# Delta rule in blocks of 64 columns on alternating halves of TensorE, with TensorE in program order

## The chip, the cores and the metric

One core of one Trainium2 chip runs the whole program. The metric is the device time of one execution in microseconds (us), lower is better.

## The reference

Batch 1, 512 tokens, width 1024, float32. A first block of two layers (MLA attention and gated linear attention) is followed by a second block of two layers; the change lies only in the mixer of the second block. Cut to what it computes there:

```python
proj = h @ w_in                                  # h = rms_norm(x)
# dilated attention over 8 heads of 64: three patterns, merged by softmax of their log sums
# delta rule: 4 heads, dk = dv = 128, chunks C = 64, N = 8 chunks
qkv = silu(causal_dwconv(dn_qkv, dn_conv_w))     # q, k, v of the delta rule
beta = sigmoid(dn_b); g = -exp(a_log) * softplus(dn_a + dt_bias)
q = q * rsqrt(sum(q*q) + EPS) * K**-0.5;  k = k * rsqrt(sum(k*k) + EPS)
g = cumsum(g, -1)                                # within each chunk of 64
decay = exp(where(tril, g_i - g_j, -inf))
A = where(strict, (beta k) k^T * decay, 0);  T = (I + A)^-1
u = T @ (v * beta);  w = T @ (beta * k * exp(g));  qk = (q k^T) * decay
for each chunk:                                  # state is 128 x 128 a head
    v_new = u_i - w_i @ state
    o = (q_i * exp(g)) @ state + qk_i @ v_new
    state = state * exp(g_last) + (k_i * exp(g_last - g))^T @ v_new
mix = concat([attn, rms_norm(o) * silu(z)]) @ w_out
```

## The kernel before

**Dense work.** Each large product is done as three fp32r matmuls per 128x128x512 block (`mm3`, L178 to L181: high times high, low times high, high times low), eight blocks deep. The weights come over SP's DMA queue (`wr<-in_w`, L140), are rounded by ACT (L143) and their rest taken by DVE (L144). `t_out` gives a 128-column slice with the channels on the partitions, `n_out` a 128-token slice with the tokens there.

**The mixer `mix2`**, once per layer: z projections (`ev`), the log decays (L948, L949 and what leads to them), then the **main stage**: k, q and v of the four heads with `t_out` (`dn`), their convolution and silu (`conv_silu_`, ACT and DVE), the attention's q and k with `n_out` and rope, and its v (`v_rows`). Between these dense matmuls lie the small f32 groups of the delta rule. TensorE takes an f32 matmul as two passes, and the trace counts passes. The groups, for each head four 128x128 tiles (a tile holds two chunks on its diagonal, the rest is masked away):

- `gB` (L1011), running decays; `G` (L1020), k times k; A goes to HBM (`dA`, L1025).
- 16x16 diagonal blocks of all heads come back in one layout (L1037), DVE inverts them in 30 steps (L1043, L1045), they go to `dT` (L1047). These DMAs are ACT's.
- `q_rows`: ACT squares all of q (L1053), TensorE sums over the partitions against a column of ones (L1056), then q times k (L1060). Both groups write bank 3 ("tr").
- `merges`: T is loaded (L1109) and flipped (L1114), then two rounds of X = A'T (L1120) and T -= T X (L1125); u (L1129) and w (L1137).
- the scan over 8 chunks: `pv` (L1151), `qv` (L1154), `dS` (L1160), one half of a tile's 128 rows or columns at a time, all four heads on the same half; `po` (L1167) once in two chunks.

**The attention stage** follows: `scores` (L1220, L1221), softmax on DVE and ACT, `weigh` (flip of the weights), `values` (L1243, two heads in turn on the two column halves), `finish`, `project`. The products of two of the four `v_rows` are issued here ("ps_mo").

**What sets the order.** The Tile scheduler orders each engine's instructions by the priorities that the program gives: `flush` runs postponed small work (`late`) at the priority of that place, the whole of `merges` stands 600 steps ahead, `scores` at its own place. So single dense matmuls stand between, and inside, the small groups.

Of the kernel before, what the change touches and what calls it, by code (L numbers as in the profile page):

```python
# [37 lines left out]
def shape_consts():  # L38
# [5 lines left out]
    for d in (3, 2, 1, 0):  # L44
# [10 lines left out]
    m16 = (i // 32 == j // 32) & (i % 32 >= 16) & (j % 32 < 16)  # L55
    m32 = same & (i % 64 >= 32) & (j % 64 < 32)
# [3 lines left out]
        "mask_ls": np.where(same & (i > j), 0.0, NEG),  # L60
        "mask_u": np.where(same & (i <= j), 0.0, NEG),
# [29 lines left out]
def body(ctx, tc, a, out, plan, n1=LAYERS, n2=LAYERS, dbg=None):  # L91
# [115 lines left out]

    def n_out(w, xk, c, evac, k_outer=False, then={}):
        nk = len(w)
        if k_outer:  # L210
            pss = [bank("mm") for _ in range(NT)]
            for k in range(nk):
                for t in range(NT):
                    mm3(pss[t][:, :c], cut(xk[k], tsl(t)), w[k], k == 0, k == nk - 1)
            for t in range(NT):
                evac(t, pss[t])
            return
        for t in range(NT):
            ps = bank("mm")
            for k in range(nk):  # L220
                mm3(ps[:, :c], cut(xk[k], tsl(t)), w[k], k == 0, k == nk - 1)
            if late:
                late.pop(0)()
            evac(t, ps)
            if t in then:
                then[t]()

    def t_out(w, xk, evac):
        nk = len(w)
        ps = bank("mm")  # L230
        for k in range(nk):
            mm3(ps, w[k], xk[k], k == 0, k == nk - 1)
        flush()
# [620 lines left out]
    def z_w(l, j):  # L854
        return take_n("w_in_2", l, np.concatenate([rng2(6)[j * 256:j * 256 + 256], rng2(7 + j)]), range(KT))

    def block2(xt, xd, pss):
        with ExitStack() as c2:
# [15 lines left out]
            dA = [dr.tile([P, 4, SEQ], F32, name=f"dA{l}", bufs=1) for l in range(LAYERS)]  # L874
            dT = [dr.tile([P, 4, SEQ], F32, name=f"dT{l}", bufs=1) for l in range(LAYERS)]
            zt = tmp()
            nc.gpsimd.memset(zt, 0.0)
            for l in range(n2):
                for h in range(4):
                    nc.sync.dma_start(dT[l][:, h], zt)  # L880
# [5 lines left out]
    def mix2(l, rt, xt, par, row, dA, dT, pss):  # L886
# [3 lines left out]
        with ExitStack() as cm:  # L890
            pm = pool(f"pm{l}", cm)
            deal(mm=(0, 1, 2), tr=(3,), d=(4, 5, 6, 7), pv=(4,), qv=(5,), dS=(6,), po=(7,),
# [10 lines left out]
            def dt():  # L903
                return gt("dt", 6)
# [4 lines left out]
            def f16(ap):  # L909
                return ap.rearrange("p h t -> p (h t)")  # L910

# [8 lines left out]
            for j in range(2):  # L920
                def ev(t, ps, j=j):
                    zs = z[t][:, tsl(j, 256)]
                    silu2(ps[:, :256], zs, 256)
                    nc.vector.scalar_tensor_tensor(heads(zs, 2), heads(zs, 2), 0.5, mid(d_gain, 2), ALU.mult, ALU.mult)
                    nc.vector.tensor_copy((bb, aa)[j][:, :, t], ps[:, 256:260])
# [21 lines left out]
            ps = bank("d")  # L947
            nc.tensor.matmul(ps[:, 0:16], cc("tri"), f16(graw), start=True, stop=True)  # L948
            nc.tensor.matmul(ps[:, 16:32], cc("same"), f16(graw), start=True, stop=True)  # L949
            gc, ngc, kd, eg = s16("gc"), s16("ngc"), s16("kd"), s16("eg")  # L950
            nc.vector.tensor_copy(f16(gc), ps[:, 0:16])
            nc.vector.tensor_scalar(f16(ngc), ps[:, 0:16], -1.0, None, ALU.mult)
            nc.vector.tensor_tensor(f16(kd), ps[:, 16:32], f16(gc), ALU.subtract)
            nc.scalar.activation(kd, kd, AF.Exp)
            nc.scalar.activation(eg, gc, AF.Exp)


            def conv_silu(m, ps, dst):
                with tc.high_priority(offset=0):
                    conv_silu_(m, ps, dst)  # L960

            def conv_silu_(m, ps, dst):
# [7 lines left out]
                nc.vector.scalar_tensor_tensor(dst, th, 1.0, acc, ALU.add, ALU.mult)  # L970
# [15 lines left out]
            A, ET, kN, qT = rows(set4("A")), rows(set4("ET")), rows(set4("kN")), rows(set4("qT"))  # L986
            kT = [gt("kT", 4) for _ in range(4)]
# [14 lines left out]
            for h in range(4):  # L1002
                dn(4 + h, kT[h])
                late.append(lambda h=h: k_rows(h))


            decl = pm.tile([P, 4, 8], F32, name="decl")
            for h in range(4):
                gB = bank("d")
                for t in range(NT):  # L1010
                    nc.tensor.matmul(gB[:, tsl(t)], graw[:, h, t:t + 1].to_broadcast([P, P]), cc("tri"),  # L1011
                                     start=True, stop=True)
                nc.scalar.activation(decl[:, h], gB.rearrange("p (n c) -> p n c", c=64)[:, :, 63], AF.Exp)
                d = dt()
                nc.vector.scalar_tensor_tensor(v4(d), v4(gB), -1.0, mid(cc("mask_ls"), NT), ALU.mult, ALU.add)
                nc.vector.tensor_tensor(v4(ET[h]), v4(gB), mid(cc("mask_u"), NT), ALU.add)
                flush()
                G = bank("d")
                for t in range(NT):
                    nc.tensor.matmul(G[:, tsl(t)], kT[h][:, tsl(t)], kT[h][:, tsl(t)], start=True, stop=True)  # L1020
                for t in range(NT):
                    nc.scalar.activation(d[:, tsl(t)], d[:, tsl(t)], AF.Exp, bias=gc[:, h, t:t + 1])
                    nc.vector.scalar_tensor_tensor(A[h][:, tsl(t)], G[:, tsl(t)], sa[:, h, t:t + 1], d[:, tsl(t)],
                                                   ALU.mult, ALU.mult)
                nc.scalar.dma_start(dA[:, h], A[h])  # L1025
                for t in range(NT):
                    nc.scalar.activation(ET[h][:, tsl(t)], ET[h][:, tsl(t)], AF.Exp, bias=ngc[:, h, t:t + 1])


            def diag(d, u):  # L1030
                row_ = 4 * SEQ
                return bass.AP(d.tensor, d.offset + u * (16 * row_ + 16), [[P, 16], [row_, 16], [1, 16]])

            LR = dt().rearrange("p (b r c) -> p b r c", b=2, r=16)
            Lb, Rb = LR[:, 0], LR[:, 1]
            for u in range(8):
                nc.scalar.dma_start(Lb[16 * u:16 * u + 16], diag(dA, u))  # L1037
            nc.sync.dma_start(Rb, a["eye16"])
            tmpb = tmp(256).rearrange("p (r c) -> p r c", r=16)
            for j in range(15):  # L1040
                n = 15 - j
                tv = tmpb[:, :n, :j + 1]
                nc.vector.tensor_tensor(tv, Lb[:, j + 1:, j:j + 1].to_broadcast([P, n, j + 1]),  # L1043
                                        Rb[:, j:j + 1, :j + 1].to_broadcast([P, n, j + 1]), ALU.mult)
                nc.vector.tensor_tensor(Rb[:, j + 1:, :j + 1], Rb[:, j + 1:, :j + 1], tv, ALU.subtract)  # L1045
            for u in range(8):
                nc.scalar.dma_start(diag(dT, u), Rb[16 * u:16 * u + 16])  # L1047
# [3 lines left out]
            def q_rows(h):  # L1051
# [3 lines left out]
                for t in range(NT):  # L1055
# [396 lines left out]
```

## Time and profile before

| | |
|---|---|
| median of 3 runs | 2131.49 us (2128.54 to 2132.91) |
| the profiled execution | 2130.51 us, of which the span of the trace 2128.4 us |
| PE busy | 2037.4 us (96%) |
| PE weight loads | 1685.4 us (79%) |
| DVE, ACT, POOL busy | 1279.2 (60%), 959.2 (45%), 194.9 us (9%) |
| mean DMA rate | 98 GB/s |
| granted TensorE clock, mean | 0.996 |

TensorE is busy in nearly all of the span, the other engines in about half. The records of single matmuls overlap, so this document takes the time of a group of matmuls from its first start to the start of what follows it.

### The profile page before, as it was taken

How to read it: one execution, taken by the hardware profiler on the slowest of the kernel's cores; microseconds unless marked ns; L12 is line 12 of the kernel's file. 1: busy time of each engine (PE TensorE's matmuls, PEld its weight loads, DVE VectorE, ACT ScalarE, POOL GpSimd, SP SyncE). 2: the span in 40 equal slices, each digit the busy share in tenths (PEclk: the TensorE clock that was granted, in tenths of full speed). 3: DMA queues.
4: the chain of work that ended last, by engine and by line, in shares of the span. 5: the costliest groups of instructions: out<-in, count | busy, mean ns of one | idle time of the engine just before them, and what ended most of it. 6: DMA issues, size and time to landing. Idle time of an engine off the chain costs nothing.

```text
span 2128.4 us, 28253 instructions
## 1 busy us (share of the span) xinstructions
PE 2037.4 (96%) x10792; PEld 1685.4 (79%) x10792; DVE 1279.2 (60%) x2218; ACT 959.2 (45%) x1805; POOL 194.9 (9%) x337
## 2 busy tenths in 40 slices
PE   7899999999999899999999999999999999999998
PEld 6687878778877888777788888878887678888886
DVE  6667655667844676575666425567757646662364
ACT  4745444635634553255544324346333654442342
POOL 1110001111000111200200000021112020000001
PEclk9999999999999999999999999999999999999999
DMA  5232233322133531141633333243211244332332
GB/s 170 85 92 70 70 109 118 104 80 87 44 127 103 173 95 58 45 114 51 188 109 99 92 96 99 70 152 113 79 55 50 75 146 142 99 97 92 99 99 89
DMA packets 74038, 209.41 MB, mean 98 GB/s; under 512 B 16624, under 2 KB 17648, under 8 KB 73392
## 3 DMA queue, kind: packets, MB, share of 16 engines
q1 hardware_dynamic: 62896, 202.89, 31.1%
q10 hardware_dynamic: 11008, 4.72, 0.9%
q8 instruction: 85, 1.39, 0.3%
q14 instruction: 49, 0.40, 0.1%
HBM read 182.16 MB, written 17.04 MB: 94 GB/s over the span
## 4 chain that ended last, share of the span: by engine, by line
PE 75%; DVE 7%; ACT 6%; DMA 5%; issue 3%; POOL 3%; POOLq 0%; SPq 0%; ACTq 0%; DVEq 0%
PE ps_mm L180 19%; PE ps_mm L181 18%; PE ps_mm L179 18%; DMA wr<-in_w 4%; DVE wl L144 2%; PE ps_tr L274 2%; ACT wh L143 2%; PE ps_o L1243 1%; ACT xn L296 1%; PE ps_mo L179 1%; PE ps_mo L180 1%; PE ps_pt L274 1%; PE ps_mo L181 1%; POOL r2h L297 1%; PE ps_pv L1151 1%
## 5 line engine op out<-in xcount | busy, mean ns | idle before, releaser
L144 DVE TENSOR_TENSOR wl<-wr,wh 128x1024 fp32r<-128x1024 f32 (+4 forms) x304 | 360.7, 1189 | 395.4 <-ACT wh L143 389.7
L143 ACT CAST wh<-wr 128x1024 fp32r<-128x1024 f32 (+4 forms) x304 | 309.3, 1019 | 357.1 <-PE ps_mm L181 151.3
L180 PE MATMUL ps_mm<-wl,xh 128*128 128x512 f32 (+2 forms) x736 | 282.6, 385 | 9.3 <-DVE wl L144 9.2
L181 PE MATMUL ps_mm<-x2h,wl 128*128 128x512 f32 (+1 forms) x768 | 285.5, 372 | 0.0
L180 PE MATMUL ps_mm<-x2l,wh 128*128 128x512 f32 (+1 forms) x768 | 285.4, 372 | 0.0
L179 PE MATMUL ps_mm<-x2h,wh 128*128 128x512 f32 (+1 forms) x768 | 285.4, 372 | 0.0
L179 PE MATMUL ps_mm<-wh,xh 128*128 128x512 f32 (+2 forms) x736 | 282.7, 386 | 2.1 <-ACT wh L143 1.7
L181 PE MATMUL ps_mm<-wh,xl 128*128 128x512 f32 (+2 forms) x736 | 280.9, 382 | 0.0
L180 PEld LDWEIGHTS ps_mm<-wl,xh 128*128 128x128 f32 x736 | 139.9, 190 | 37.5 <-DVE wl L144 15.0
L181 PEld LDWEIGHTS ps_mm<-x2h,wl 128*128 128x128 f32 x768 | 144.7, 188 | 25.1
L180 PEld LDWEIGHTS ps_mm<-x2l,wh 128*128 128x128 f32 x768 | 144.7, 188 | 25.0
L179 PEld LDWEIGHTS ps_mm<-x2h,wh 128*128 128x128 f32 x768 | 144.7, 188 | 24.9
L179 PEld LDWEIGHTS ps_mm<-wh,xh 128*128 128x128 f32 x736 | 139.5, 190 | 28.8 <-ACT wh L143 4.8
L181 PEld LDWEIGHTS ps_mm<-wh,xl 128*128 128x128 f32 x736 | 139.7, 190 | 23.3 <-issue 0.7
L1336 DVE SCALAR_TENSOR_TENSOR rt<-ps_mm,par,rt 128x511 f32<-128x511 f32 (+1 forms) x176 | 131.3, 746 | 3.0
L179 PE MATMUL ps_mm<-xh,wh 128*128 128x512 f32 x320 | 127.0, 397 | 0.9 <-DVE rp L358 0.9
L180 PE MATMUL ps_mm<-xl,wh 128*128 128x512 f32 x320 | 126.4, 395 | 0.0
L181 PE MATMUL ps_mm<-xh,wl 128*128 128x512 f32 x320 | 126.4, 395 | 0.0
L297 POOL TENSOR_SCALAR r2h<-ss 128x1 f32<-128x1 f32 x48 | 18.9, 393 | 995.0 <-ACT th L296 759.6
L180 PE MATMUL ps_mm<-wl,hh 128*128 128x512 f32 x224 | 89.1, 399 | 0.6 <-DVE wl L144 0.5
L179 PE MATMUL ps_mm<-wh,hh 128*128 128x512 f32 x224 | 88.2, 395 | 0.3 <-ACT wh L143 0.3
L181 PE MATMUL ps_mm<-wh,hl 128*128 128x512 f32 x224 | 88.0, 394 | 0.0
(401 smaller groups left out, 3798.3 us busy)
## 6 DMA issues: line engine op xcount, KB each, us to landing
wr<-in_w SPq DMA_DIRECT2D x270, 512.0 KB, 3.6
gain<-in_gain SPq DMA_DIRECT2D x13, 512.0 KB, 6.3
wr<-in_w SPq DMA_DIRECT2D x14, 384.0 KB, 3.1
x<-in_x SPq DMA_DIRECT2D x8, 512.0 KB, 5.9
wm<-gqk SPq DMA_DIRECT2D x32, 128.0 KB, 2.3
xd<-x SPq DMA_DIRECT2D x8, 512.0 KB, 2.6
xs<-xd SPq DMA_DIRECT2D x8, 512.0 KB, 3.9
xs<-xm SPq DMA_DIRECT2D x8, 512.0 KB, 4.6
```

The lines of the kernel that those rows point to most:

```text
L143: nc.scalar.copy(hi[:, :n], raw[:, :n])
L144: nc.vector.tensor_tensor(lo[:, :n], raw[:, :n], hi[:, :n].bitcast(F32), ALU.subtract)
L179: nc.tensor.matmul(ps, l[0], r[0], start=start, stop=False)
L180: nc.tensor.matmul(ps, l[0], r[1], start=False, stop=False)
L181: nc.tensor.matmul(ps, l[1], r[0], start=False, stop=stop)
L274: nc.tensor.transpose(ps[:w, tsl(j)], src[:, tsl(j, w)], ident)
L296: nc.scalar.activation(junk[i], halves[i], AF.Square, accum_out=ss[:, i:i + 1])
L297: nc.gpsimd.tensor_scalar(r[:, i:i + 1], ss[:, i:i + 1], 1.0 / D, r[:, 0:1] if i else EPS, ALU.mult, ALU.add)
L1151: nc.tensor.matmul(pv[rs, tsl(h)], wT[h][:, cs], S[:, h], start=True, stop=True)
L1243: nc.tensor.matmul(o[tsl(h % 2, 64), tsl(h // 2)], av[:, j, tsl(h, 64)], p_[:, tsl(i * c + j)], start=j == 0, stop=j == qt)
L1336: nc.vector.scalar_tensor_tensor(acc[:, j:], ps[:, :SEQ - j], par[:, w0 + 3 * m + 2 - j:w0 + 3 * m + 3 - j], acc[:, j:], ALU.mult, ALU.add)
```

## The change

All of it lies in `mix2`, in both layers. PE's order is the program's own there (`manual_schedule`): `later(n, fn)` postpones a small group until n more blocks of three dense matmuls have been issued, `tick` counts them, `settle` drains the list. The delta rule uses 64x64 blocks: heads 0 and 1 keep their time halves, heads 2 and 3 have the two halves of each tile swapped, so that two heads' blocks can lie on different halves of the array. Consecutive matmuls of a group take turns between the half F (partitions 0 to 63) and B (64 to 127), most with a PSUM bank for each half. The log decays become two accumulating 64-column matmuls per block; T is written and loaded in both orientations (16 DMAs in place of 8, on SP's queue, as all of the inversion's), so it is no longer flipped after loading; the sum of q's squares is taken by flipping q and four accumulating Squares of ACT; all four `v_rows` lie in the main stage; the attention's units start their second step one unit later, and take `w_out` and the flips of the delta rule's output earlier.

```diff
+    def later(n, fn):
+        steps.append([n, fn])
+    def tick():
+        for s in steps:
+            s[0] -= 1
...
             for k in range(nk):
                 mm3(ps[:, :c], cut(xk[k], tsl(t)), w[k], k == 0, k == nk - 1)
+                tick()
...
+            cm.enter_context(tc.manual_schedule(engines={mybir.EngineType.PE}))
-            deal(mm=(0, 1, 2), tr=(3,), d=(4, 5, 6, 7), pv=(4,), qv=(5,), dS=(6,), po=(7,),
+            deal(mm=(0, 1, 2), tr=(3,), d=(4, 5, 6, 7), pv=(4,), qv=(5,), dS=(6, 7), po=(3,),
...
+            later(6, decays)
...
+            def log_decays(g):
+                M = bank("d")
+                for i in range(8):
+                    h, t, o = 2 * g + i // NT, i % NT, M[:, tsl(i, 64)]
+                    for p in HF:
+                        nc.tensor.matmul(o[p], ngraw[:, h, t:t + 1].to_broadcast([P, 64]), tri[:, p], start=True, stop=False)
+                    for p in HF:
+                        nc.tensor.matmul(o[p], tri[:, p], graw[:, h, t:t + 1].to_broadcast([P, 64]), start=False, stop=True)
...
+            def k_scores(g):
...
+                        nc.tensor.matmul(G[p, tsl(i, 64)], kc, kc, start=True, stop=True)
...
+                for d, b in zip(dT, (Rb, Lb)):
+                    for u in range(8):
+                        nc.sync.dma_start(diag(d, u), b[16 * u:16 * u + 16])
+                merge_start()
...
             def q_rows(h):
-                sq = tmp()
-                nc.scalar.activation(sq, qT[h], AF.Square)
-                ps = bank("tr")
+                sq, ps = tmp(), flip(qT[h])
                 for t in range(NT):
-                    nc.tensor.matmul(ps[:, t:t + 1], sq[:, tsl(t)], ones[:, 0:1], start=True, stop=True)
-                nc.vector.tensor_copy(ssq[:, h], ps[:, 0:NT])
-                ps = bank("tr")
+                    nc.scalar.activation(sq[:, tsl(t)], ps[:, tsl(t)], AF.Square, accum_out=ssq[:, h, t:t + 1])
+                ps = bank("tr")[:, :256]
                 for t in range(NT):
-                    nc.tensor.matmul(ps[:, tsl(t)], kT[h][:, tsl(t)], qT[h][:, tsl(t)], start=True, stop=True)
+                    for u, p in enumerate(HF):
+                        nc.tensor.matmul(ps[p, tsl(t, 64)], chunks(kT[h])[:, t, u], chunks(qT[h])[:, t, u],
+                                         start=True, stop=True)
...
+            def halves(f):
+                ps = bank("d"), bank("d")
+                for i in range(8):
+                    for p, b in zip(HF, ps):
+                        f(i, p, b)
+                return tuple(zip(HF, ps))
...
+                def left(A_):
+                    for p, ps in halves(lambda i, p, b: nc.tensor.matmul(
+                            b[p, tsl(i, 64)], A_[p, tsl(i, 64)], TT[p, tsl(i, 64)], start=True, stop=True)):
+                        nc.scalar.copy(X[p], ps[p])
...
+                for i, fn in enumerate((lambda: left(As[0]), right, turn, lambda: left(As[1]), last, values_, keys)):
+                    later(wait + 4 * i, fn)
...
+            order = [(g, 2 * g + j) for j in range(2) for g in range(2)]
...
+                for g, h in order:
+                    nc.tensor.matmul(pv[HF[u ^ g], tsl(h)], chunks(wT_[:, h])[:, t, u ^ g], S[:, h], start=True, stop=True)
...
+                    later(2, lambda: update(n))
...
+                later(3, lambda: chunk(n + 1))
...
+            k_heads()
+            for h in range(4):
+                dn(h, qT[h])
+                later(10, lambda h=h: q_rows(h))
...
-            D1, D2, IW = 2, 5, 9
-            IV = [2 + 2 * i for i in range(NT - 2)]
-            IO = range(6, 6 + 4)
+            D1, D2, IW = 3, 5, 0
+            IO = range(2, 2 + NT)
```

In the changed code the three dense lines are L181 to L183, and flips are L298. The order of PE's instructions in three places (one row is one kind of matmul; an f32 one counts once here, and as two passes in the trace):

The rows of q for one head in the main stage, before (`ps_tr` is bank 3, `th` the squares):

```order
L1056 MATMUL ps_tr<-ones,th 128x1 x4
L180 MATMUL ps_mm<-xl,wh 128x512
L181 MATMUL ps_mm<-xh,wl 128x512
L179 MATMUL ps_mm<-xh,wh 128x512
L180 MATMUL ps_mm<-xl,wh 128x512
L181 MATMUL ps_mm<-xh,wl 128x512
L1060 MATMUL ps_tr<-qT,kT 128x128 x4
```

and now:

```order
L182 MATMUL ps_mm<-xl,wh 128x512
L183 MATMUL ps_mm<-xh,wl 128x512
L298 MATMUL ps_tr<-ident,qT 128x128 x4
L1145 MATMUL ps_tr<-qT,kT 64x64 x8
L181 MATMUL ps_mm<-xh,wh 128x512
```

The two groups on bank 3 were five dense matmuls apart, and now follow each other.

One step of the scan, before (`ps_dS` is the state's update, `ps_pv` and `ps_qv` the products with the state; dense ones stand between):

```order
L1160 MATMUL ps_dS<-vn,kN 128x128 x4
L181 MATMUL ps_mm<-wh,xl 128x512
L179 MATMUL ps_mm<-wh,xh 128x512
L180 MATMUL ps_mm<-wl,xh 128x512
L181 MATMUL ps_mm<-wh,xl 128x512
L1151 MATMUL ps_pv<-S,A 64x128 x4
L1154 MATMUL ps_qv<-S,qT 64x128 x4
```

and now:

```order
L1278 MATMUL ps_pv<-S,A 64x128 x4
L1283 MATMUL ps_qv<-S,qT 64x128 x4
L181 MATMUL ps_mm<-wh,xh 128x512
L182 MATMUL ps_mm<-wl,xh 128x512
L183 MATMUL ps_mm<-wh,xl 128x512
L298 MATMUL ps_tr<-ident,cv 128x128 x4
L181 MATMUL ps_mm<-wh,xh 128x512
L182 MATMUL ps_mm<-wl,xh 128x512
L183 MATMUL ps_mm<-wh,xl 128x512
L1298 MATMUL ps_dS<-vn,kN 128x128 x4
```

The groups keep their size; whole blocks of three dense matmuls stand between them.

The first units of the attention, before (`ps_s` are scores, `ps_pt` flipped weights, `ps_mo` the attention's v of tokens 256 to 511):

```order
L181 MATMUL ps_mo<-wh,xl 128x512
L179 MATMUL ps_mo<-wh,xh 128x512
L180 MATMUL ps_mo<-wl,xh 128x512
L274 MATMUL ps_pt<-ident,dt 128x128
L181 MATMUL ps_mo<-wh,xl 128x512
L179 MATMUL ps_mo<-wh,xh 128x512
L180 MATMUL ps_mo<-wl,xh 128x512
L1220 MATMUL ps_s<-ET,qT 128x256
L181 MATMUL ps_mo<-wh,xl 128x512
```

and now:

```order
L1389 MATMUL ps_s<-kN,A 128x256
L1390 MATMUL ps_s<-vs,A 128x256
L1389 MATMUL ps_s<-ET,qT 128x256
L1390 MATMUL ps_s<-lo,qT 128x256
L298 MATMUL ps_po<-ident,uN 128x128 x4
L1389 MATMUL ps_s<-kN,A 128x256
L1390 MATMUL ps_s<-vs,A 128x256
L1389 MATMUL ps_s<-ET,qT 128x256
L1390 MATMUL ps_s<-lo,qT 128x256
L298 MATMUL ps_pt<-ident,dt 128x128 x2
```

No dense matmul is left between the first scores.

## Rows read from the trace of the kernel before

**Rows 1.** The page: busy time and share of the span of each engine.

```profile
PE 2037.4 (96%) x10792; PEld 1685.4 (79%) x10792; DVE 1279.2 (60%) x2218; ACT 959.2 (45%) x1805; POOL 194.9 (9%) x337
```

**Rows 2.** Stretches: main and attention stage of layer 0, main of 1, the attention's start.

```profile
core 0: us, PE busy (x) PEld busy (x) DVE busy (x) ACT busy (x) POOL busy (x), PEclk, DMA share, GB/s
733.00:935.00 202.00, 195.28 (x1144) 163.19 (x1145) 137.80 (x254) 84.20 (x176) 33.53 (x39) 1.00 0.24 72
935.00:1012.00 77.00, 74.07 (x467) 56.47 (x466) 44.98 (x145) 45.41 (x112) 0.19 (x1) 1.00 0.31 84
1446.70:1642.00 195.30, 190.02 (x1115) 158.24 (x1116) 136.33 (x250) 80.59 (x173) 34.83 (x39) 1.00 0.22 66
...
940.00:960.00 20.00, 17.17 (x99) 12.72 (x97) 12.87 (x57) 13.85 (x40) 0.00 (x0) 1.00 0.52 138
```

**Rows 3.** Timeline of PE, full-width groups: start, us, line, tiles, passes.

```profile
826.27 1.13 PE L1120 MATMUL ps_d<-dt 128*128 128x128 f32 x8
827.15 0.47 PE L180 MATMUL ps_mm<-wl,xh 128*128 128x512 f32 x1
...
830.45 0.60 PE L274 MATMUL ps_d<-ident,dt 128*128 128x128 f32 x4
830.88 1.06 PE L1120 MATMUL ps_d<-dt 128*128 128x128 f32 x8
```

**Rows 4.** Timeline of PE: sums of q's squares against ones, and dense matmuls behind.

```profile
789.03 0.95 PE L1056 MATMUL ps_tr<-ones,th 128*128 128x1 f32 x8
789.84 0.48 PE L180 MATMUL ps_mm<-xl,wh 128*128 128x512 f32 x1
790.15 0.39 PE L181 MATMUL ps_mm<-xh,wl 128*128 128x512 f32 x1
790.38 0.40 PE L179 MATMUL ps_mm<-xh,wh 128*128 128x512 f32 x1
```

**Rows 5.** Timeline of PE: the scan, all heads on one half.

```profile
876.82 1.16 PE L1160 MATMUL ps_dS<-vn,kN 64*128 64x128 f32 x8
877.90 0.50 PE L181 MATMUL ps_mm<-wh,xl 128*128 128x512 f32 x1
878.24 0.40 PE L179 MATMUL ps_mm<-wh,xh 128*128 128x512 f32 x1
...
879.03 1.09 PE L1151 MATMUL ps_pv<-S,A 128*64 128x128 f32 x8
879.96 1.04 PE L1154 MATMUL ps_qv<-S,qT 128*64 128x128 f32 x8
880.92 0.50 PE L179 MATMUL ps_mm<-wh,xh 128*128 128x512 f32 x1
```

**Rows 6.** Timeline of PE, first block: matmuls that take turns between row halves.

```profile
80.66 0.27 PE L547 MATMUL ps_sf<-wm 64*128 64x128 f32 x1
80.67 0.27 PE L547 MATMUL ps_sb<-wm 64*128 64x128 f32 x1
80.77 0.27 PE L547 MATMUL ps_sf<-wm 64*128 64x128 f32 x1
```

**Rows 7.** Timeline of PE, attention: turns between column halves.

```profile
993.85 1.09 PE L1243 MATMUL ps_o<-cv,av 128*64 128x128 f32 x16
994.88 0.50 PE L1220 MATMUL ps_s<-ET,qT 128*128 128x512 f32 x1
```

**Rows 8.** Timeline of ACT: a weight cast, and the first Squares of k's rows.

```profile
746.12 1.05 ACT L143 CAST wh<-wr 128x1024 fp32r<-128x1024 f32 x1 [0.63 <-PE ps_mm L180]
...
748.74 0.31 ACT L996 ACTIVATE th<-kN 128x128 f32<-128x128 f32 x1
...
749.05 0.29 ACT L996 ACTIVATE th<-kN 128x128 f32<-128x128 f32 x1
```

**Rows 9.** Timeline: PE at the decays; DVE at the inversion's first step.

```profile
733.31 0.37 PE L948 MATMUL ps_d<-graw,cst 128*128 128x16 f32 x2 [1.20 <-issue]
...
782.17 0.19 DVE L1043 TENSOR_TENSOR th<-dt 128x15 f32<-128x15 f32 x1 [0.72 <-DMA dt<-dA]
```

More of the change, by code (lines that the diff above doesn't have):

```diff
@@ L984, in rows @@
                 return [ap[:, i] for i in range(4)]
[L986 to L987 removed]
+            wT_, ET_, kN, qT = set4("A"), set4("ET"), rows(set4("kN")), rows(set4("qT"))
+            nc.gpsimd.memset(ET_, 0.0)
+            kT = rows(set4("kT"))
+            EA = set4("lo")
+            E, A = EA[:, 0:2], EA[:, 2:4]
             ssk, ssq = s16("ssk"), s16("ssq")
@@ new lines, in values_ @@
+                def values_():
+                    for j in range(2):
+                        h = 2 * g + j
+                        ps = bank("d"), bank("d")
+                        for t in range(NT):
+                            for p, b in zip(HF, ps):
+                                nc.tensor.matmul(b[p, tsl(t)], TT[p, tsl(NT * j + t, 64)], vs[h][p, tsl(t)],
+                                                 start=True, stop=True)
+                        for p, b in zip(HF, ps):
+                            nc.scalar.copy(uN[0][p, :, tsl(h)], v4(b[p]))
@@ new lines, in keys @@
+                def keys():
+                    for u, (p, ps) in enumerate(halves(lambda i, p, b: nc.tensor.matmul(
+                            b[:, tsl(i, 64)], kN[2 * g + i // NT][p, tsl(i % NT)], Tk[p, tsl(i, 64)],
+                            start=True, stop=True))):
+                        for j in range(2):
+                            nc.scalar.activation(chunks(wT_[:, 2 * g + j])[:, :, u], b64(ps[:, tsl(j, 256)]), AF.Copy,
+                                                 scale=-1.0)
+                    for h in (2 * g, 2 * g + 1):
+                        nc.vector.tensor_tensor(v4(kN[h]), v4(kN[h]), end(kd[:, h], P), ALU.mult)
+                    if g:
+                        later(3, scan_start)
@@ new lines, in update @@
+            def update(n):
+                t, u = n // 2, n % 2
+                vn, S_ = vns[t], Ss[n + 1]
+                dS = bank("dS"), bank("dS")
+                for g, h in order:
+                    p = HF[u ^ g]
+                    nc.tensor.matmul(dS[g][:, tsl(h % 2)], kN[h][p, tsl(t)], vn[p, tsl(h)], start=True, stop=True)
+                for g in range(2):
+                    Sg = S_[:, 2 * g:2 * g + 2]
+                    nc.vector.tensor_tensor(Sg, Sg, heads(dS[g][:, :256], 2), ALU.add)
+                if u == 0 and t:
+                    delta_norm(t - 1)
+                later(3, lambda: chunk(n + 1))
@@ new lines, in delta_norm @@
+            def delta_norm(t):
+                oN = uN[0][:, t]
+                po = bank("po")
+                for h in range(4):
+                    nc.tensor.matmul(po[:, tsl(h)], ET_[:, h, tsl(t)], vns[t][:, tsl(h)], start=True, stop=True)
+                nc.vector.tensor_tensor(oN, oN, po, ALU.add)
+                sq = dt()
+                nc.scalar.activation(sq, oN, AF.Square)
+                ss = sml.tile([P, 4], F32, tag="ss4", name="ss4")
+                nc.vector.tensor_reduce(ss, v4(sq), AX.X, ALU.add)
+                nc.vector.tensor_tensor(ss, ss, cq2[:, :, t], ALU.mult)
+                r = rstd(ss, 4, 1.0 / P)
+                r2 = sml.tile([P, 4], F32, tag="r2", name="r2")
+                nc.vector.tensor_tensor(r2, r[:, :4], cq[:, :, t], ALU.mult)
+                nc.vector.tensor_tensor(v4(oN), v4(oN), end(r2, P), ALU.mult)
+                nc.vector.tensor_tensor(oN, oN, z[t], ALU.mult)
+                if t == NT - 1:
+                    operands()
@@ L1202, in mix2 @@
+            w_v.extend(take_n("w_in_2", l, rng(2), range(KT)))
+            for t in range(NT):
+                v_rows(t)
+            settle()
+            yt.extend(act_tiles())
             lead[0] = 5
```

378 lines of the change are left out of this document (203 added, 175 removed).

## Prediction

> **What bounds the kernel now.** The page first: TensorE is busy in 96% of the span, the other engines in 60% and less [rows 1]; so what counts is time on PE, and only waits that PE itself takes. Then the stretches: the change lies in a main stage of 202.0 us and an attention stage of 77.0 us in layer 0, and their like in layer 1 (195.3 us for the main stage). PE stands still for 202.0 - 195.3 = 6.7 us in the first main stage and 195.3 - 190.0 = 5.3 us in the second; the granted clock is full (1.00) in all of them [rows 2], so it has nothing to give back. Last the timeline of PE, for what each small group really takes, from its first start to the start of what follows; the durations in the rows are longer, because passes overlap. The sum is made for one layer, doubled, and set against the profiled execution's own 2130.5 us; the median of the runs is 1.0 us above that.
>
> **What the removed groups take.** A group of four full-width f32 matmuls, eight passes, takes 827.15 - 826.27 = 0.88 us [rows 3]. A layer has 36 such groups that change: four each of L1011, L1020, L1060, L1129 and L1137, eight each of L1120 and L1125: 31.7 us. The four sums against ones take 789.84 - 789.03 = 0.81 us each [rows 4], 3.2 us. The eight flips of T take 830.88 - 830.45 = 0.43 us each [rows 3], 3.4 us. In the scan eight `pv` take 879.96 - 879.03 = 0.93, eight `qv` 0.96, seven `dS` 877.90 - 876.82 = 1.08 us [rows 5]: 22.7 us. Together **61.0 us**.
>
> **What the new groups take.** The scan's `pv` and `qv` now take turns between column halves, with shapes that the attention's `values` already has: 16 passes in 994.88 - 993.85 = 1.03 us [rows 7]. Eight pairs of groups cost 8.2 us. For seven `dS` of eight passes I take 0.6 us each, a little over half of that: 4.2 us. So the scan falls from 22.7 to 12.4 us. `values_` and `keys` are 64 passes each of mixed halves, at 1.03 / 16 = 0.065 us a pass 4.1 us each. Flips of q and the turns of T are eight groups of four, at 0.43 us 3.4 us. The decays have 12 passes in place of 4, at 0.1 us 0.8 us more.
>
> What is left is new in kind: 512 passes of 64x64 blocks with 64 moving columns (log decays 128, k times k 64, q times k 64, `left` and `right` 256), in 16 groups; they replace 28 full-width groups. No row shows such a pass. From one side: on row halves of 128 columns a pair starts together and the next 0.11 us later [rows 6], 0.055 us a pass; a weight of half the columns on each half, if the cost goes with the columns, makes 0.027. From the other: on column halves of 64, with twice the moving columns, a pass takes about 0.054 us [rows 7], if 0.17 us of the group goes into coming and going. And one moving column costs nearly what 128 do, 0.81 against 0.88 us for eight passes [rows 3, 4], so fewer moving columns alone buy little. Both halves' rows fit a cost that goes with the weights' columns, two halves side by side; I take **0.035 us**, nearer to the low end, because a quarter block uses both a row half and a column half, and keep 0.027 and 0.054 for the range. 512 x 0.035 = 17.9 us, and 16 x 0.2 = 3.2 us for coming and going (a dense matmul behind a half group takes 878.24 - 877.90 = 0.34 us, behind another dense one 790.38 - 790.15 = 0.23 [rows 4, 5], and something is lost on the way in). Together 8.2 + 4.2 + 8.2 + 3.4 + 0.8 + 17.9 + 3.2 = **45.9 us**. The saving is **15.1 us a layer**; 19.2 at 0.027, 5.4 at 0.054.
>
> **What the new order costs.** PE has one order now, and whatever stands late in it stops the dense work too.
>
> *q's rows.* The flip of q and the product of q and k are neighbours on PE and both write bank 3; the second must wait until ACT has squared the first out of it. Four Squares start 0.31 us apart [rows 8], 1.2 us; a flip group's record runs 0.2 us beyond its share, 0.60 against 0.43 [rows 3]; and ACT, busy 84.2 of 202.0 us [rows 2], is sometimes in a cast of 1.05 us [rows 8]. I take 2.0 us a head, **8.0 us a layer**; between 1.3 (ACT idle) and 3.1 (behind a whole cast). Before, five dense matmuls lay between the two groups, and the squares came from SBUF. Behind the waiting product stand only dense matmuls, so all of it is lost.
>
> *Decays.* PE waited 1.20 us there already [rows 9]. It now arrives two dense matmuls, 0.5 us, earlier, and the chain ahead has some small DVE operations more, for the swapped halves, for which I give 0.7 us: **1.2 us** more, between 0 and 3.
>
> *Inversion.* SP's queue gets the writes of A, the gathers of the diagonal and both writes of T, with weight loads queued behind them; DVE's 30 steps, that began at 782.17 behind the gather [rows 9], stand in one piece, with q's convolutions behind, which wait as long as DVE waits for the gather. The first consumer of T comes 46 blocks after, at least 46 x 3 x 0.23 = 32 us, so that T itself is in time; what can be late is q's data at its rows. **2 us**, between 0 and 5.
>
> *Attention.* The two `v_rows` cost the same in the main stage, 48 x 0.23 = 11.0 us, but no longer fill waits. In 940 to 960 us PE is busy 17.2, ACT 13.9 and DVE 12.9 us [rows 2]: with most of that filler gone PE has some 9 us of work against ACT's 14. One part of the 5 us is got back by the longer distance D1 and by fewer single dense matmuls that each pay for coming and going: **2.5 us**, between -1 and 6.
>
> *At nothing* I cost z's evacuation in halves and the flips of the delta rule's output split in three: more instructions of DVE and ACT, beside dense matmuls that fill PE; if that cover goes, they are tenths of a us each. The operands of the attention (casts, differences and four DMAs) are asked for when the last chunk is normalised and the last k is turned, with most of four `v_rows`, 4 x 24 x 0.23 = 22 us, still to run on PE; if they are late, the first scores are.
>
> *Waits that go.* Of the 5 to 7 us that PE now idles in the main stage I let **2.5 us** go, since groups stand at distances chosen by hand: between 0 and 5.
>
> **Sum.** 15.1 - 8.0 - 1.2 - 2.0 - 2.5 + 2.5 = 3.9 us a layer, 7.8 for both: 2130.5 - 7.8 = 2122.7, and as a median **2123.7 us**. About 0.2%, 4.3 us, is what a measurement of this kernel can tell from no change.
>
> **Rivals.**
>
> *A small pass costs what a larger one does.* Then halving the block doubles the passes for nothing: at 0.054 us the saving is 5.4 us, less than the 11.2 us that the order costs (all the terms below the saving): 5.8 us lost a layer, **2143 us**. It decides from 0.043 us a pass on: the 45.9 us without their 17.9 are 28.0, and 61.0 - 28.0 - 512 x 0.043 leaves 11 us. For it speaks the row with one moving column; against it that quarter blocks lie on different rows and different columns. The Trainium skill, TensorEngine Tiling (Array Packing), section Instruction Overhead, says that each matmul has an overhead of about 60 cycles, that a free dimension of 1 takes as long as one of 60, and that one shouldn't tile a dimension that is already small. By that rule this rival holds; the trace agrees for a full-width weight (0.81 against 0.88 us).
>
> *PE waits in its fixed order.* If each product of q and k waits 3.1 us, and late operands hold PE at the other places as much as their upper bounds (inversion 5, attention 6), the order costs 12.4 + 1.2 + 5 + 6 - 2.5 = 22.1 us against 15.1: 7 us lost a layer, **2145.5 us**. It decides from 15.1 us a layer on, where I have 11.2. For it: a scheduler's order lets dense matmuls slip into a gap, a fixed one doesn't. Against it: most groups have their operands many blocks ahead.
>
> *Halves wholly in parallel, waits at their least.* 19.2 - 5.2 - 0.6 - 1.0 - 1.0 + 2.5 = 13.9 us a layer: **2103.7 us**. For it: the pairs that start together [rows 6].
>
> *The two sides cancel.* With 0.04 us a pass and the waits as I have them the sum is 15.1 - 2.6 - 11.2 = 1.3 us a layer, and the time within 4 us of before: the blocks do what they are for, and the order eats it.
>
> **How the numbers follow.** My forecast (a pass between 0.03 and 0.04 us, waits near the middle; 2115 to 2129 us) has 0.42, of which 0.07 lies within 0.2%; small passes at a fixed cost 0.20; waits in the order 0.15; wholly parallel 0.13; cancelling 0.10. Faster: 0.35 + 0.13, and 0.01 of the cancelling case: 0.49. Same: 0.07 + 0.09 and 0.01 of the slower ones' near ends: 0.17. Slower: 0.34. The range reaches from the wholly parallel case to the waits' one, 2103 to 2147 us; what lies beyond needs both ends of two unknowns at once.
>
> **What would show it.** In the changed profile a group of `left` or `right`, 32 passes, should take about 32 x 0.035 + 0.2 = 1.3 us; 1.9 or more is the first rival. `pv` and `qv` together should take 1.0 to 1.1 us instead of 1.9. The product of q and k (L1145) should stand 1.3 to 3.1 us idle behind ACT's Square, eight times. The idle time at the decays should be above 2 us. The attention's first 20 us should show PE below 17 us busy. The forecast is wrong in its mechanism if the small groups don't shrink by some 15 us a layer, or if a wait I have not named takes over 3 us a layer: weights late behind SP's new DMAs, or DVE late with a convolution.

## The result, and the profile after

The changed kernel takes 2205.37 us (median of 4 runs, 2197.81 to 2206.9) against 2132.2 us before: 1.034 times as long, 95% interval 1.031 to 1.037. It is slower by 73 us, and outside the range. The page of the changed kernel (busy engines, then the granted clock in tenths, in 40 slices):

```profile
PE 2040.2 (93%) x11448; PEld 1675.4 (76%) x11448; DVE 1289.4 (58%) x2282; ACT 953.0 (43%) x1807; POOL 185.2 (8%) x331
...
PEclk9999999999999889988999999998799899999999
```

PE is 93% busy and not 96 [rows 1], and the clock, full before in the stretches of [rows 2], has lost tenths in both mixers. The busy time has hardly grown (2040.2 us against 2037.4): in the sum over the kernel, what came is idle time.

The timeline of PE in the main stage of layer 0, only the rows of q (L1145 is the product of q and k; in brackets the wait and who ended it):

```profile
796.28 1.12 PE L1145 MATMUL ps_tr<-qT,kT 128*64 128x64 f32 x16 [11.14 <-ACT th L1141]
...
809.15 0.69 PE L1145 MATMUL ps_tr<-qT,kT 128*64 128x64 f32 x16 [4.48 <-ACT th L1141]
...
822.02 1.12 PE L1145 MATMUL ps_tr<-qT,kT 128*64 128x64 f32 x16 [4.47 <-ACT th L1141]
...
835.60 1.12 PE L1145 MATMUL ps_tr<-qT,kT 128*64 128x64 f32 x16 [4.47 <-ACT th L1141]
```

That is 24.6 us in this layer; the same four places take 24.0 us in the other. Who keeps ACT from the Squares (L1141) is in its own timeline and DVE's, before the third wait:

```profile
816.51 0.68 ACT L1028 ACTIVATE cv<-ps_mm,half_w 128x512 f32<-128x512 f32 x1
...
817.89 2.32 DVE L1030 SCALAR_TENSOR_TENSOR cv<-ps_mm,half_w,cv 128x511 f32<-128x511 f32 x3
820.30 0.63 ACT L1033 ACTIVATE th<-cv 128x512 f32<-128x512 f32 x1 [3.12 <-DVE cv L1030]
820.84 0.26 ACT L1141 ACTIVATE th<-ps_tr 128x128 f32<-128x128 f32 x1
```

Ten blocks after its unit, the next unit (eight blocks) has just ended, and its tanh (L1033) stands in ACT's queue ahead of the Squares. ACT waits 3.1 us for DVE's convolution, with the Squares behind it and PE behind these. At the first head the tanh had already run, and the Squares themselves waited 5.3 us for DVE's last step of that convolution (L1035), which stood behind the inversion's first steps, and these behind the gather:

```profile
793.54 0.18 DVE L1127 TENSOR_TENSOR th<-dt 128x15 f32<-128x15 f32 x1 [4.48 <-DMA dt<-dA]
...
795.09 0.28 ACT L1141 ACTIVATE th<-ps_tr 128x128 f32<-128x128 f32 x1 [5.30 <-DVE qT L1035]
```

By the code the tanhs, the Squares and the inversion share two scratch buffers (`th`), so the Squares have to wait until DVE has read the tanh; no run gave them buffers of their own, so this part of the 11.1 us is argued.

Behind such a wait the clock is down to its lower level, 1.2 GHz: dense matmuls that follow each other by 0.23 us [rows 4] take 824.51 - 824.09 = 0.42 us, and the granted clock of the stretch is 0.50 (the last line: its ends, its length, busy time and count of PE, PEld, DVE, ACT and POOL, granted clock, DMA share and GB/s):

```profile
824.09 0.63 PE L183 MATMUL ps_mm<-xh,wl 128*128 128x512 f32 x1
824.51 0.63 PE L181 MATMUL ps_mm<-xh,wh 128*128 128x512 f32 x1
...
823.07:826.65 3.58, 3.58 (x11) 2.81 (x9) 1.09 (x4) 0.00 (x0) 0.27 (x1) 0.50 0.00 0
```

The new groups, in the same view, are as short as was hoped: 32 passes of `left` in 853.69 - 852.61 = 1.08 us, `pv` with `qv` in 917.44 - 916.42 = 1.02 us where they took 1.89 [rows 5]:

```profile
852.61 1.15 PE L1212 MATMUL ps_d<-dt 64*64 64x64 f32 x32
853.69 0.50 PE L181 MATMUL ps_mm<-xh,wh 128*128 128x512 f32 x1
...
916.42 0.66 PE L1278 MATMUL ps_pv<-S,A 128*64 128x128 f32 x8
916.91 0.61 PE L1283 MATMUL ps_qv<-S,qT 128*64 128x128 f32 x8
917.44 0.50 PE L181 MATMUL ps_mm<-wh,xh 128*128 128x512 f32 x1
```

In the attention PE waits for the flips of the delta rule's output, four in a row on one bank, each behind its evacuation in three pieces, and for the second head's scores, which share a bank with the first's:

```profile
983.38 0.63 PE L298 MATMUL ps_po<-ident,uN 128*128 128x128 f32 x4 [2.31 <-DVE xl L288]
...
984.77 0.58 PE L1389 MATMUL ps_s<-ET,qT 128*128 128x256 f32 x1 [0.53 <-DVE mx L1394]
```

In the same form as above, the attention's first 20 us and all of it: PE stands still for 79.0 - 65.5 = 13.5 us, where before it was 77.0 - 74.1 = 2.9 us [rows 2].

```profile
975.00:995.00 20.00, 9.88 (x48) 7.18 (x46) 13.09 (x61) 12.04 (x42) 0.00 (x0) 0.73 0.32 101
975.00:1054.00 79.00, 65.51 (x420) 50.83 (x419) 41.11 (x149) 41.90 (x115) 0.19 (x1) 0.87 0.17 56
```

At the end of the main stage the flips of the rope's output wait too, once for bank 3, which the scan's `po` shares, and once for the rope itself on DVE (L382), where it stands among the steps of the delta rule's norm. Both waits come again in the second layer, 1.30 and 3.48 us there as well:

```profile
945.77 0.66 PE L298 MATMUL ps_tr<-ident,cv 128*128 128x128 f32 x4 [1.30 <-DVE uN L1312]
...
956.12 0.63 PE L298 MATMUL ps_tr<-ident,cv 128*128 128x128 f32 x4 [3.48 <-DVE cv L382]
```

The ledger of one mixer (layer 0, from the start of the last z matmul of the first half to the start of what follows the last of `project`, worked out from all of PE's timeline rows there; the attention's small matmuls count among the small ones):

| us | mixer | idle | dense | small |
|---|---|---|---|---|
| before | 293.5 | 10.3 | 172.6 | 110.6 |
| changed | 335.2 | 49.6 | 187.4 | 98.2 |

Idle 39.3 us more, dense 14.8 us more for the same matmuls (the clock), small 12.4 us less, part of them at the lower clock. In the profiled executions the spans differ by 2205.1 - 2128.4 = 76.7 us, so the second layer loses some 35 us; a wait of 3.2 us at the z stage is in the first alone.

### The profile page after: what moved, and what is told of

Same layout as the page of the kernel before. It is cut to its first block, busy times and chain, and to the rows that moved or that the text cites. A ratio compares the mean times of both kernels' runs of the same rounds, so it can differ in the third digit from the quotient of the medians.

```text
span 2205.1 us, 29619 instructions
## 1 busy us (share of the span) xinstructions
PE 2040.2 (93%) x11448; PEld 1675.4 (76%) x11448; DVE 1289.4 (58%) x2282; ACT 953.0 (43%) x1807; POOL 185.2 (8%) x331
## 4 chain that ended last, share of the span: by engine, by line
PE 42%; DVE 3%; ACT 2%; DMA 1%; POOL 1%; issue 1%; SPq 0%; POOLq 0%; DVEq 0%; ACTq 0%
PE ps_mm L181 12%; PE ps_mm L182 12%; PE ps_mm L183 12%; DMA wr<-in_w 1%; DVE wl L146 1%; ACT wh L145 1%; DVE cv L1030 1%; PE ps_tr L298 1%; PE ps_o L1412 0%; POOL r2h L321 0%; PE ps_s L1389 0%; PE ps_pt L298 0%; POOL r2o L323 0%; PE ps_mo L181 0%; PE ps_mo L183 0%
## 5 line engine op out<-in xcount | busy, mean ns | idle before, releaser
L181 PE MATMUL ps_mm<-wh,xh 128*128 128x512 f32 (+2 forms) x768 | 302.3, 395 | 5.6 <-DVE ea L992 3.5
L182 PE MATMUL ps_mm<-wl,xh 128*128 128x512 f32 (+2 forms) x768 | 295.2, 385 | 8.6 <-DVE wl L146 8.3
L183 PE MATMUL ps_mm<-wh,xl 128*128 128x512 f32 (+2 forms) x768 | 294.3, 384 | 0.0
L183 PE MATMUL ps_mm<-x2h,wl 128*128 128x512 f32 (+1 forms) x768 | 285.5, 372 | 0.0
L181 PE MATMUL ps_mm<-x2h,wh 128*128 128x512 f32 (+1 forms) x768 | 285.4, 372 | 0.0
L182 PEld LDWEIGHTS ps_mm<-wl,xh 128*128 128x128 f32 x768 | 147.7, 192 | 37.2 <-DVE wl L146 14.4
L181 PEld LDWEIGHTS ps_mm<-wh,xh 128*128 128x128 f32 x768 | 147.6, 193 | 37.2 <-issue 7.4
L183 PEld LDWEIGHTS ps_mm<-wh,xl 128*128 128x128 f32 x768 | 147.7, 192 | 25.9
L181 PEld LDWEIGHTS ps_mm<-x2h,wh 128*128 128x128 f32 x768 | 144.7, 188 | 25.1
L183 PEld LDWEIGHTS ps_mm<-x2h,wl 128*128 128x128 f32 x768 | 144.7, 188 | 25.1
L181 PE MATMUL ps_mm<-xh,wh 128*128 128x512 f32 x320 | 137.8, 431 | 0.9 <-DVE rp L382 0.9
L182 PE MATMUL ps_mm<-xl,wh 128*128 128x512 f32 x320 | 132.6, 414 | 0.0
L183 PE MATMUL ps_mm<-xh,wl 128*128 128x512 f32 x320 | 132.4, 414 | 0.0
L181 PE MATMUL ps_mm<-wh,hh 128*128 128x512 f32 x224 | 88.1, 395 | 0.1
L183 PE MATMUL ps_mm<-wh,hl 128*128 128x512 f32 x224 | 87.8, 394 | 0.0
L181 PEld LDWEIGHTS ps_mm<-xh,wh 128*128 128x128 f32 x320 | 65.3, 204 | 16.4 <-ACT th L310 1.2
```

Of the source, the lines that this page charges most:

```text
L181: nc.tensor.matmul(ps, l[0], r[0], start=start, stop=False)
L182: nc.tensor.matmul(ps, l[0], r[1], start=False, stop=False)
L183: nc.tensor.matmul(ps, l[1], r[0], start=False, stop=stop)
```

## The experiments

Times are medians; the kernel before ran beside each, at 2131 us. Code cuts are marked by three dots.

**e1_own_bank.** What has to wait for bank 3?

```diff
-                ps = bank("tr")[:, :256]
+                ps = bank("d")[:, :256]
```

> Edit: the product of q and k takes a bank of the four 'd' banks, no longer bank 3, so PE need not wait for the Squares that read the flip of q out of bank 3. Theory A (the stop is bank 3, with the Squares queued on ACT behind the next unit's tanh, which waits for DVE's convolution): the four waits of 11.1, 4.5, 4.5 and 4.5 us before L1145 in layer 0 go, with them the half-clock stretches behind them (dense matmuls there cost some 14 us a layer more than before): 2205 - 2 x (24.6 + 10 to 14) = 2128 to 2136 us. Theory B (the late thing is the inversion on DVE, bank 3 only shows it): the first 11 us move to the next flip of q and only the three shorter waits go: 2205 - 2 x (13.4 + 7) = about 2164 us.

2159.07 us, ratio 1.014 (1.012 to 1.016): 46 of the 73 us from one bank. It lies between A and B, nearer B: the three waits of 4.5 us are gone, of the 11.1 us half is left at the next flip, which now waits for bank 3 and so for the same Squares:

```profile
795.15 1.12 PE L298 MATMUL ps_tr<-ident,qT 128*128 128x128 f32 x4 [5.57 <-ACT th L1141]
```

**e2_seven.** Is it the place in ACT's queue?

```diff
-                later(10, lambda h=h: q_rows(h))
+                later(7, lambda h=h: q_rows(h))
```

> Edit: q's rows are due 7 blocks after their unit and not 10, so that their Squares are queued on ACT ahead of the next unit's convolution; bank 3 stays shared. Theory A: each of the four waits falls from 4.5 us (and 11.1) to the 1.5 to 2.0 us that four Squares take on a free ACT, some 7 us a layer in all: 2205 - 2 x (17 + 8) = about 2155 us, and L1145 still idle behind ACT. If the place in ACT's queue is not the cause, the waits stay at 4.5 us and the time at 2205.

2187.03 us (ratio 1.028). That lies between the two expected times. Ahead of the next tanh the Squares cost PE 1.2 to 1.3 us a head, so the place in the queue is what made 4.5 of it. The rest of the gain is eaten by a new wait: seven blocks are too few for the second q, whose convolution stands on DVE behind the inversion. (The fourth q is late too, by 2.7 us.)

```profile
798.23 1.09 PE L298 MATMUL ps_tr<-ident,qT 128*128 128x128 f32 x4 [12.69 <-DVE dt L1129]
800.55 1.12 PE L1145 MATMUL ps_tr<-qT,kT 128*64 128x64 f32 x16 [1.23 <-ACT th L1141]
```

**e3_attention** and **e4_both.** The attention as before, alone and with e1.

```diff
-            for t in range(NT):
+            for t in range(2):
                 v_rows(t)
...
-            D1, D2, IW = 3, 5, 0
-            IO = range(2, 2 + NT)
+            D1, D2, IW = 2, 5, 9
+            IV = [2 + 2 * i for i in range(NT - 2)]
+            IO = range(6, 6 + 4)
...
+                if i in IV:
+                    v_rows(2 + IV.index(i), "mo")
...
-                ps = flip(uN[0][:, t], role="po")
+                ps = flip(uN[0][:, t], role="mo")
```

> Edit: the attention stage as before the change (two of the v_rows back in it, second step after 2 units, w_out at unit 9, delta rule's flips at units 6 to 9, those in the two 'mo' banks since bank 3 holds the sums of values there); the main stage else as changed. Theory: the attention's 13.3 us of idle time on PE fall to about 3 and its clock comes back: 2 x (10 + 3) less, about 2179 us (2172 to 2190). Rival (the attention's waits are set by DVE and ACT whatever PE does): no gain, 2205.

> Edit: both, the product in its own bank and the attention as before. If the two losses are independent, the gains add: about 2105 us (2100 to 2118), under the kernel before; if one hides the other, not below 2128.

2201.36 and 2152.03 us: 4 us less than the changed kernel and 7 less than e1, not 26. The 4 us lie within the scatter of the runs (2199.65 to 2203.5 against 2197.81 to 2206.9). The attention's waits named above are gone, but with two `v_rows` less ahead of them the first scores now wait for the operands' DMAs, 5.7 us in layer 0 of e3:

```profile
966.30 0.35 PE L1390 MATMUL ps_s<-vs,A 128*128 128x256 f32 x1 [1.71 <-DMA vs<-vs]
...
968.80 0.55 PE L1389 MATMUL ps_s<-ET,qT 128*128 128x256 f32 x1 [2.15 <-DMA ET<-ET]
...
971.14 0.58 PE L1390 MATMUL ps_s<-lo,qT 128*128 128x256 f32 x1 [1.79 <-DMA lo<-lo]
```

So the four `v_rows` in the main stage are what hides the operands, and the attention pays for it: by the ledger's count PE idles 49.3 us in this mixer of e3, and 49.6 in the changed kernel.

**e6_one_half.** Does taking turns make the passes cheap, or their size?

```diff
-                for i in range(8):
-                    for p, b in zip(HF, ps):
+                for p, b in zip(HF, ps):
+                    for i in range(8):
                         f(i, p, b)
```

The same swap is made in k times k and in `values_` and `keys`, and the scan's order of heads is changed with it.

> Edit on e1: the same passes, but in each group all of one half first and then all of the other (left and right, k times k, values, keys, scan). If taking turns is what makes a pass cheap: a group of 32 passes of left goes from 1.08 to 1.7 us (0.054 a pass) or more, the scan's pv and qv from 1.0 to 1.9, dS from 0.64 to 1.08: 20 to 25 us a layer, 2159 + 40 to 50 = about 2200 us. If the small blocks alone make it cheap: no change in the groups, 2159.

2187.85 us, 29 us over e1. A group of 32 passes takes 842.77 - 840.95 = 1.82 us, 0.057 a pass, with turns 0.034. So the turns make it, and the price with turns is the forecast's 0.035. The scan's groups hardly moved (0.50 and 0.58 us): in their new order two heads follow on one half and then two on the other, so the 40 to 50 us didn't come. Why one change of half after four passes is enough there, and one after sixteen is not in `left`, no run shows.

```profile
840.95 1.90 PE L1212 MATMUL ps_d<-dt,lo 64*64 64x64 f32 x32
842.77 0.50 PE L181 MATMUL ps_mm<-wh,xh 128*128 128x512 f32 x1
```

`left` has weights of 64 rows and 64 columns (64*64 in the row), so its turns change both the row half and the column half, and it gives each half a bank of its own. k times k (L1105) has 128 rows and 64 columns (128*64), changes the column half alone and writes both into one bank. Its 32 passes cost the same: 779.64 - 778.56 = 1.08 us with turns (the changed kernel) and 776.98 - 775.15 = 1.83 us without (e6). So there at least neither a second bank nor a change of row half is needed:

```profile
778.56 1.15 PE L1105 MATMUL ps_d<-kT 128*64 128x64 f32 x32
779.64 0.50 PE L181 MATMUL ps_mm<-xh,wh 128*128 128x512 f32 x1
```

```profile
775.15 1.90 PE L1105 MATMUL ps_d<-kT 128*64 128x64 f32 x32
776.98 0.50 PE L181 MATMUL ps_mm<-xh,wh 128*128 128x512 f32 x1
```

**e7_pad.** What does the clock take, apart from the waits?

```diff
+                pad = bank("d")
+                for _ in range(18):
+                    nc.tensor.matmul(pad, xk[0][0][:, :P], xk[0][0], start=True, stop=True)
                 ps = bank("tr")[:, :256]
```

> Edit on the changed kernel: 18 dense matmuls whose result nobody reads stand between each flip of q and the product that waits for bank 3, so PE works through the wait of 4.5 us (all but 7 us of the first). The waits stay as long, so what is won is the clock alone: if PE's lower clock behind the waits is a loss of its own, the dense matmuls behind L1145 take 0.23 us again and the time falls by 10 to 25 us (2180 to 2195); if the clock costs nothing, 2205.

2198.21 us: 7 us less, under the 10 to 25 expected, and the runs of the two overlap (2195.25 to 2199.51 against 2197.81 to 2206.9). What shows the clock as a loss of its own are stretches of 20 us, of the changed kernel and of e7 (columns as above):

```profile
805.00:825.00 20.00, 11.38 (x65) 9.11 (x66) 10.48 (x19) 4.95 (x20) 7.50 (x8) 0.80 0.44 117
825.00:845.00 20.00, 15.53 (x71) 12.44 (x70) 6.41 (x10) 4.93 (x13) 1.20 (x2) 0.78 0.09 27
```

```profile
805.00:825.00 20.00, 18.70 (x112) 14.88 (x111) 11.78 (x20) 4.96 (x20) 7.56 (x8) 1.00 0.44 117
825.00:845.00 20.00, 19.66 (x115) 15.76 (x115) 10.09 (x16) 6.80 (x16) 1.20 (x2) 1.00 0.16 54
```

The padding holds the clock at 1.00 there; in the mixer of layer 0 the dense matmuls take 181.1 us instead of 187.4. The first head's wait was padded in part (PE still idles 6.9 us there), and the attention not at all; that the rest over 172.6 lies behind these is likely, not shown.

**e8_main** and **e5_spread.** Every wait of e1 that has a name, put off or given a bank: e8 in the main stage alone, e5 in the attention too.

```diff
-            banks["mm"] = (0, 1, 2, 4, 5, 6, 7)
+            banks["mm"] = (5, 6, 7, 0, 1, 2, 4)
+            turn["mm"] = -1
...
-            later(6, decays)
+            later(9, decays)
...
-                    later(7, turned)
+                    later(10, turned)
...
-                later(10, lambda h=h: q_rows(h))
+                later(18 if h else 12, lambda h=h: q_rows(h))
```

> Edit on e1: as e5 without its edits of the attention. The difference to e5 is the attention's share. Expected: 2159 less 2 x (5.6 + 4.5 + 2.1 + 1) less 3 = about 2130 us (2124 to 2140).

> Edit on e1: the flips of q are due 12 (first head) and 18 blocks after their unit, so that the convolution delayed by the inversion is ready; the decays after 9 blocks and not 6; the flips of the rope after 10 and not 7; the z stage takes the free banks 5 to 7 first; the last v_rows is spread over the attention's first eight units, one block a unit; the flips of the delta rule's output go to a bank of their own at units 4 to 7, w_out at unit 7. Theory (what is left of the loss is PE waiting in a fixed order at named places, plus the clock): e1's 2159 less per layer 5.6 (flip of q), 4.5 (rope), 2.1 (decays), 8 of the attention's 11, some 3 of clock, and 3 once for z: about 2110 us (2100 to 2125), under the kernel before. Rival (DVE's total work bounds these places): the waits move to other places and it stays at 2150.

2141.87 us (ratio 1.005, 1.003 to 1.007), just above the expected range, and 2134.06 us (1.0012, 1.0002 to 1.0022), between theory and rival: nearly level with the kernel before, not under it. In layer 0 flips of q and of v still wait for bank 3 (2.7 and 5.2 us in both runs), and in e5, with a `v_rows` less in the main stage, the operands' DMAs are late again (4.1 us).

**e9_banks, e10_later, e11_fill, e12_pool.** Four steps on, e9 from e5, e10 from e9, e11 and e12 from e10: banks for the flips of q, half of the filler back; T used later and the merges and the scan pulled together; more filler in the attention; q and v later still, and part of the norm on POOL.

```diff
-                sq, ps = tmp(), flip(qT[h])
+                sq, ps = tmp(), flip(qT[h], role="d")
...
-                    merge(g, 46 + 2 * g)
+                    merge(g, 54 + 2 * g)
...
-                    later(wait + 4 * i, fn)
+                    later(wait + 3 * i, fn)
...
-                later(3, lambda: chunk(n + 1))
+                later(2, lambda: chunk(n + 1))
```

(The first pair is e9's, the others e10's.)

> Edit on e5: the flips of q go to the four 'd' banks too, so that neither they nor the flips of v wait for Squares; the rows of the second q are due 18 blocks after its unit, of the other three 12, those of the first k 13 and not 10; the rope's flips 9; four blocks of the last v_rows return to the main stage, and the other four stand between the two heads of the attention's first units. Theory: e5 still loses per layer 2.7 + 5.2 us at flips behind bank 3, 1.9 at the first flip of k, 4.1 at the operands' DMAs and some 2 between the heads, with some 3 of clock behind them: 2134 less 2 x (7.9 + 1.5 + 3 + 1 + 3) = about 2101 us (2095 to 2118), under the kernel before by 0.6 to 1.7%. Rival (DVE's work sets the pace of these stages, the waits only move): 2125 to 2134, no better than before.

> Edit on e9: T's first use is due 54 blocks after the inversion's last DMA is issued and not 46, the steps of the merges 3 blocks apart and not 4, a chunk's start 2 blocks behind the update and not 3, so the scan ends no later. Theory: e9 still waits 6.5 us a layer for T's load at its first use, a wait that came up because PE arrives earlier; with dense work in its place and its share of the clock 2 x (6.5 + 2) less: 2134 - 17 = 2117 us (2108 to 2125). Rival (the chain through DVE and the DMAs from the inversion to the attention's operands is what bounds the stage): the wait moves on to the merges, the scan or the first scores, 2128 to 2136.

> Edit on e10: all eight blocks of the last v_rows between the two heads of the attention's first eight units, none in the main stage. Theory: e9's attention stands still for 5 us at the second head's scores and runs at 0.83 of the clock over 40 us; with twice the filler both shrink: some 5 us a layer under e10, if the operands are in time; if they are not, the first scores wait some 2 to 4 us a layer for their DMAs and it equals e10.

> Edit on e10: q's rows 3 blocks later (15, the second head 21), the flips of v after 13 blocks and not 10, and the last two products of the delta rule's norm on POOL for all but the last tokens, to relieve DVE while it makes the rope and v's weights. Theory: e10's small groups are 15.6 us a layer shorter than those of the kernel before, and its PE idles 12.9 us a layer more; of that the flips of q and v wait 6.0 us for DVE and 6 to 7 us stand where DVE is full. If half to all of the 6.0 and some 2 of the rest go: 2129 less 2 x (3 to 8) = 2113 to 2123 us, under the kernel before. Rival (DVE's chain bounds the stage, so a wait put off comes up later): 2126 to 2133.

2134.22, 2129.29 (ratio 0.9992, 0.9981 to 1.0003), 2137.87 and 2141.56 us. e10 against e9 is the one step that gained; e11 and e12 are slower than e10, by 9 and 12 us. e9 took away the waits at bank 3 and e10 the one for T, and each got others; e11 got the operands' DMAs back (2.9 us in layer 0), and in e12 the flips of q and v still wait 4.8 us for DVE, 6.0 in e10. The first use of T (L1213) in e9, then in e12:

```profile
818.08 1.97 PE L1213 MATMUL ps_d<-dt 64*64 64x64 f32 x32 [6.53 <-DMA dt<-dT]
```

```profile
827.28 1.97 PE L1213 MATMUL ps_d<-dt 64*64 64x64 f32 x32 [8.21 <-DMA dt<-dT]
```

In e12 T itself is later. DVE has more of the convolutions' work between the inversion's steps, and the copy that ends the inversion (L1131) starts 814.03 - 805.32 = 8.7 us later than in e10 (first line e10, second e12):

```profile
805.32 0.38 DVE L1131 COPY dt<-dt 128x256 f32<-128x256 f32 x1
```

```profile
814.03 0.35 DVE L1131 COPY dt<-dt 128x256 f32<-128x256 f32 x1
```

e10, which waits for T no more, stands near the end of the scan: at a flip of the rope, for bank 3 that `po` shares, and at a weight's rest that DVE has yet to make (2.55 us in e9 already). No run gave `po` a bank apart from these flips.

```profile
906.95 0.66 PE L298 MATMUL ps_tr<-ident,cv 128*128 128x128 f32 x4 [2.27 <-DVE uN L1313]
...
914.88 0.50 PE L182 MATMUL ps_mm<-wl,xh 128*128 128x512 f32 x1 [2.25 <-DVE wl L146]
```

The same ledger as above: e1 312.9 us (idle 30.5, dense 183.3, small 99.1), e5 300.3 (25.0, 180.0, 95.4), e10 294.1 (23.2, 175.8, 95.0), e12 302.9 (27.6, 178.9, 96.3). In e10 the small groups are 15.6 us shorter than before, and idle is 12.9 and dense 3.2 us longer: 0.5 us is left over for the worse. All four missed what their theories promised. The rival of e9, e10 and e12, that the chain through DVE and the DMAs (inversion, merges, scan, operands) bounds the stage, fits them best: T's load, DVE's norm beside its rope, and the operands take the place of one another. It gave the time of e9 (within 0.3 us of its range) and of e10; e12 is 9 us above it. No run relieved that chain alone, so that it is the bound is argued. That no order of this kernel does better is not shown; none that I tried beats the kernel before.

## Why the prediction was wrong

- **The saving was right.** I forecast 15.1 us a layer at 0.035 us a pass; measured are 0.034 with the coming and going, and 12.4 us in the changed kernel, part of it at the lower clock, 15.6 us where the clock is nearly full (e10). The first rival (a fixed price) is out: e6 shows that it is what one gets without turns, 0.057. One premise didn't hold: half of the 512 passes, those of the log decays and of the products of k and q with k, are no quarter blocks but have 128 rows and 64 columns; k times k shows the same price for them.
- **The step that failed is the wait at q's rows.** I gave it 2.0 us a head, at most 3.1, "behind a whole cast". That bounds what ACT is busy with, not what it waits for: ahead of the Squares stood a tanh whose input DVE had yet to make, and at the first head the Squares waited for DVE themselves. Measured: 11.1, 4.5, 4.5 and 4.5 us, 24.6 us in layer 0 where I had 8.0. e1 gets 46 us back from that bank; e2, with the Squares ahead of the tanh, waits 1.23 us, about the 1.3 that I had for a free ACT.
- **The clock was left out.** I read 1.00 in [rows 2] and wrote that it had nothing to give back; that it could be lost was not in the sum. Dense work took 14.8 us more in layer 0; e7 shows that filling the waits gives some of it back.
- **The attention was too cheap.** I took 2.5 us more a layer, at most 6; PE idles 13.5 us there, 10.6 more than before. I had argued from engines' totals, and missed that four flips now stand in a row on one bank and that two heads' scores share one. The flips' evacuation in three pieces, which I had at nothing, "tenths of a us each", made PE wait 2.3, 1.5 and 1.5 us.
- **A wait that I had not named** took over 3 us a layer, my own sign that the mechanism was wrong: the flips of the rope behind DVE, 1.3 and 3.5 us in both layers. The wait of 3.2 us at the z stage, in layer 0 alone, was not named either.
- The decays came out as said (2.11 us idle where I had 2.4), and the inversion showed at the named place, the second head's q, but larger: I had 2 us, at most 5, and the flip there waits 5.6 us in e1 and 12.7 in e2.
- The second rival had the direction and the mechanism, a fixed order in which PE stands at whatever is late, but at 22 us a layer and 2145.5 us. What it lacked was the size of a wait behind another engine's wait, and the clock.

## What to carry to other kernels

When an instruction is to wait for another engine, look in that engine's queue at what stands ahead, and at what that waits for: a bound from busy times is none. In a fixed order of TensorE give two groups that follow one another, one of them read by another engine, a bank each. Small matmuls on turns of the halves saved 12 to 16 us a layer on TensorE here, but they also take away the time under which the chain on the other engines was hidden.

## What was not expected of the hardware

Passes of 64x64 blocks that take turns cost 0.034 us with 64 moving columns, about what was forecast, and 0.057 when sixteen follow one another on one half; weights of 128x64 that change the column half alone, in one bank, cost the same two prices. And the clock behind waits: 0.80 and 0.78 in the two stretches above, 0.77 in e10's attention from 940 to 960 us, where PE is busy 13.9 of 20 us, while the kernel before holds 1.00 there with 17.2 [rows 2]:

```profile
940.00:960.00 20.00, 13.91 (x66) 9.59 (x65) 14.90 (x67) 12.80 (x44) 0.00 (x0) 0.77 0.33 105
```
